# Hooks of the large products moved one product earlier inside a block

## The chip, the cores and the metric

The kernel runs on one core of a Trainium2 chip. The metric is device time in microseconds (us) of one execution; the number that counts is the median of several runs. "Fast" here means fewer microseconds, nothing else. Differences are told against the kernel before the change.

## The reference

The program is one inference step of a two-layer backbone with width 2048. It treats 128 context tokens and 128 latent tokens together, so nearly every matrix product has 256 token columns. Cut to what matters here, a layer is:

```python
mod = silu(cond) @ w_ada[l] + b_ada[l]           # shift, scale, gate, twice
h = rmsnorm(x, g_norm_mix[l]) * (1 + sc1) + sh1
m = mixer_ab(h, ...) if l % 2 == 0 else mixer_c(h, ...)   # attention, in and out products
x = x + gt1 * m
h = rmsnorm(x, g_norm_ffn[l]) * (1 + sc2) + sh2
x = x + gt2 * conv_ffn(h, ...)                   # w_up 2048 x 11264, w_down 5632 x 2048
```

Layer 0 has the mixer of two head groups, layer 1 the differential attention (`mixer_c`). All weights are float32 and are read once from device memory.

## The kernel before, in words

Tokens lie in the columns and features in the partitions. A large product is made block column by block column: 128 output features at a time, over `KD = 16` blocks `k` of 128 input features, all added up in one PSUM tile `acc`. For precision every operand is split into a high and a low part in the type fp32r. The weights come by DMA as `raw` tiles of 1 MB; ScalarE writes the high part `wh` (L237) and VectorE the low part `wl` (L238). The inputs `hx`, `hxc` or `u` hold their high part `xh(k)` and low part `xl(k)` side by side. One block `k` is thus three matmuls: `wh.xh`, `wh.xl` and `wl.xh`. In the profile's rows the first two read the tile `wh` and the third reads `wl`; all of TensorE's matmuls bear the line L104 of a helper, its transposes L107, so they are told apart by tile names.

`gemm` writes these 48 matmuls of one output block. It takes an argument `between`: a function, called at block 8 of 16, or a table from block number to function. What such a hook issues stands in the middle of a block's three matmuls. Where `between` is given, all the matmuls of the product are kept in the order in which they are written (`keep_order`); hooks issue their own TensorE instructions into the same order. There are three users:

- `modulated`, called three times, makes the first three block columns of the next large product out of inputs that are not normalised yet (`u`, 258 columns wide: the two extra ones carry the shift). Its hooks are the sums of the norm (`stats`, at block 6 of the first product: four matmuls into an `att` tile), the spreading of the resulting factor over all partitions (`factor`, block 13 of the first), and the two halves of one unit of the `w_ada` product (`sums(0)` at block 6 of the second product, `sums(2)` at block 13 of the third: 8 matmuls each out of two `araw` tiles).
- `ffn` passes a table for its first products; one of them holds a hook with the four transposes that end such a unit (`misc<-am`).
- `mixer_c` passes `middle` with each of its projections. It pumps one step of whatever is due: the scores of a head (`att<-dk,dq`), transposes, the products with the values (`att<-dv,pT`), rows of `w_ada` (`ada<-araw`), and side sums on VectorE (`aacc<-block`, L481) whose 256 KB tiles `block` come over the same DMA queue (SP, L497) as the weights (SP, L284).

Instructions of the other engines are placed by a scheduler that works through a simulated timeline, under the same chain of kept orders where `keep_order` pins them. Buffers come from rotating pools: three `raw` tiles of 16 blocks, four `wh` and four `wl` halves of 8 blocks, three `acc`, three `att`, three `block`.

Of the kernel before, what the change touches and what calls it, by code (L numbers as in the profile page):

```python
# [88 lines left out]
def step_kernel(ctx: ExitStack, tc: tile.TileContext, A: dict):  # L89
# [4 lines left out]
    def keep_order(i):  # L94
        if not any(i is j for j in kept):
            kept[:] = [i]
            tc.keep_in_program_order(i)
# [16 lines left out]
    pe = TensorE()  # L114
# [20 lines left out]
    def T_(pl, shape, tag, dt=F32, bufs=None):  # L135
        kw = {} if bufs is None else {"bufs": bufs}
        return pl.tile(shape, dt, tag=tag, name=nm(tag), **kw)
# [185 lines left out]
    def gemm(blocks, xh, xl, n=NT, first=0, between=None):  # L323

        fixed = lambda i: keep_order(i) if between is not None else i
        ps = T_(pacc, [P, 512], "acc")
        last = len(blocks) - 1
        for i in range(last + 1):  # L330
            k = (i + first) % (last + 1)
            wh, wl = blocks[k]
            fixed(pe.matmul(ps[:, :n], wh, xh(k), start=(i == 0), stop=False))
            fixed(pe.matmul(ps[:, :n], wh, xl(k), start=False, stop=False))
            if callable(between):
                if i == (last + 1) // 2:
                    between()
            elif between and i in between:
                between[i]()
            fixed(pe.matmul(ps[:, :n], wl, xh(k), start=False, stop=(i == last)))  # L340
        return ps[:, :n]

# [323 lines left out]
    def modulated(st, l, which, W, u, to, rp):  # L666
# [39 lines left out]
        hooks[2][13] = lambda: sums(2)  # L706
        uh, ul = (lambda k: u[:, k, :UW]), (lambda k: u[:, k, UW:])
        ps = [gemm(W.chunk(), uh, ul, UW, between=hooks[c]) for c in range(2)]
        last = W.chunk()
        rb = got["rb"]  # L710
# [4 lines left out]
        for c in range(KD):  # L715
# [3 lines left out]
            if c in (5, 10):  # L719
                W.ahead(lambda i: i)  # L720
        ready.append(scaled(gemm(last, uh, ul, UW, between=hooks[2]), rbs))
        if which == 0:
            later.extend(steps)
# [119 lines left out]
    def mixer_ab(hx, rb0, beside):  # L843
        l = 0
        with tc.tile_pool(name="ab", bufs=1) as ab:
            with tc.tile_pool(name="abp", bufs=1) as pj:
# [105 lines left out]
                def part(W, k0, n, first, rate, between=None, then=None, **kw):  # L952

                    for c in range(23):
                        ps = gemm(W.chunk(), lambda k: hx[:, k0 + k, :NT], lambda k: hx[:, k0 + k, NT:2 * NT])
                        to = pr[:, c] if c < 11 else kvb[:, c - 11] if c < 15 else qb[:, c - 15]
                        if first:
                            act.copy(to, ps)
                        else:
                            dve.tensor_tensor(out=to, in0=to, in1=ps, op=ALU.add)  # L960
                        if between:
                            between(c)
                        pump(rate, **kw)
                        if c == 18 and then:
                            then()
# [542 lines left out]
```

## Time and profile before

| | |
|---|---|
| runs | 2368.92 us median of 3 (2361.41, 2368.92, 2373.19) |
| the profiled execution | 2368.09 us, of it 2366.2 us span from first to last instruction |
| TensorE matmul busy | 2324.9 us (98% of the span), 19666 matmuls |
| VectorE, ScalarE, GpSimd busy | 1852.1, 1191.0, 177.8 us |
| mean granted TensorE clock | 0.995 |
| DMA | 612.97 MB, mean 259 GB/s |

The stages in the profile's time, us from the start of the span: input products, heads and output product of layer 0 up to 455; first `modulated` about 455 to 492; feed-forward of layer 0 to 1180; second `modulated` to 1210; `mixer_c` to about 1500, its output product to 1604; third `modulated` to 1638; feed-forward of layer 1 to the end. A row of the timeline gives start, duration, engine, line, operation, tiles and count; "PE" is a matmul, "PEld" the load of its stationary operand.

### The profile page before, as it was taken

The page shows a single profiled execution, that of the slowest core. Times are in us where ns is not written, and L with a number is a line of the kernel's source. Part 1 is how long each engine was busy: PE and PEld are TensorE (multiplying, and loading weights), DVE is VectorE, ACT ScalarE, POOL GpSimd, SP SyncE. Part 2 cuts the span into 40 slices and gives each one's busy share as a digit, 9 for nine tenths or more (in the row PEclk, how much of TensorE's full clock was granted, in tenths as well). Part 3 has the DMA queues.
Part 4 walks back from the last instruction along what each step waited for, and adds up shares of the span by engine and source line. Part 5 has one row for each costly group of instructions (what it writes and reads, how often), then busy time and mean ns, then how long its engine had stood idle before and what let it go on. Part 6 is the DMA issues. An engine that isn't in the chain of part 4 may idle for free.

```text
span 2366.2 us, 47897 instructions
## 1 busy us (share of the span) xinstructions
PE 2324.9 (98%) x19666; PEld 2214.9 (94%) x19666; DVE 1852.1 (78%) x2864; ACT 1191.0 (50%) x1980; POOL 177.8 (8%) x242
## 2 busy tenths in 40 slices
PE   6999999999999999999999999999999999999998
PEld 4788778999999999999999999999999999999998
DVE  3569768889999999999988888787998655666644
ACT  4246455665553355554564544557555434555443
POOL 0002111210000000001130000123000000000011
PEclk9999999999999999999999999999999999999999
DMA  9988888677777777677778888667666555555553
GB/s 362 354 320 302 300 301 333 233 281 267 266 256 291 288 280 260 251 264 276 281 277 305 291 292 313 246 250 267 250 250 246 181 191 183 188 187 186 189 183 121
DMA packets 106812, 612.97 MB, mean 259 GB/s; under 512 B 11553, under 2 KB 19553, under 8 KB 38881
## 3 DMA queue, kind: packets, MB, share of 16 engines
q1 hardware_dynamic: 106592, 609.92, 70.8%
q8 instruction: 154, 2.52, 0.4%
q14 instruction: 66, 0.53, 0.1%
HBM read 605.12 MB, written 4.75 MB: 258 GB/s over the span
## 4 chain that ended last, share of the span: by engine, by line
PE 95%; DVE 2%; DMA 2%; ACT 1%; issue 0%; POOL 0%; DVEq 0%; ACTq 0%
PE acc L104 87%; PE ada L104 4%; PE att L104 2%; DMA araw<-w_ada 1%; PE att L107 1%; DVE wl L238 1%; PE misc L104 0%; PE ada L107 0%; DMA raw<-w_in_ab 0%; DVE sqacc L200 0%; DVE x L1370 0%; DMA cst<-cst 0%; ACT wh L237 0%; DVE aacc L481 0%; DMA block<-w_ada 0%
## 5 line engine op out<-in xcount | busy, mean ns | idle before, releaser
L104 PE MATMUL acc<-hx,wh 128*128 128x256 f32 (+1 forms) x7296 | 1278.8, 280 | 6.6 <-ACT hx L614 4.3
L237 ACT CAST wh<-raw 128x1024 fp32r<-128x1024 f32 (+2 forms) x824 | 793.5, 974 | 956.8 <-PE acc L104 758.5
L238 DVE TENSOR_TENSOR wl<-raw,wh 128x1024 fp32r<-128x1024 f32 (+2 forms) x824 | 920.8, 1132 | 312.3 <-ACT wh L237 309.6
L104 PEld LDWEIGHTS acc<-hx,wh 128*128 128x128 f32 x7296 | 1109.1, 188 | 37.3 <-issue 17.1
L104 PE MATMUL acc<-hx,wl 128*128 128x256 f32 (+1 forms) x3648 | 1017.2, 279 | 4.7 <-DVE wl L238 4.7
L104 PEld LDWEIGHTS acc<-hx,wl 128*128 128x128 f32 x3648 | 692.4, 190 | 7.7 <-DVE wl L238 5.9
L104 PE MATMUL acc<-g,wh 128*128 128x256 f32 x2816 | 488.2, 278 | 0.0
L104 PEld LDWEIGHTS acc<-g,wh 128*128 128x128 f32 x2816 | 426.9, 188 | 0.0
L104 PE MATMUL acc<-g,wl 128*128 128x256 f32 x1408 | 391.7, 279 | 0.0
L452 DVE CUSTOM_DVE_ANT_0 junk<-araw,condb 128x2048 f32<-128x2048 f32 x120 | 275.8, 2298 | 0.0
L104 PE MATMUL acc<-hxc,wh 128*128 128x256 f32 (+1 forms) x1536 | 267.8, 278 | 0.2 <-DVE hxc L741 0.2
L104 PEld LDWEIGHTS acc<-g,wl 128*128 128x128 f32 x1408 | 267.2, 190 | 0.0
L104 PEld LDWEIGHTS acc<-hxc,wh 128*128 128x128 f32 x1536 | 233.3, 188 | 0.7 <-DVE hxc L741 0.4
L104 PE MATMUL acc<-hxc,wl 128*128 128x256 f32 (+1 forms) x768 | 218.2, 284 | 0.0
L200 POOL TENSOR_TENSOR sqacc<-sqacc,sq 128x256 f32<-128x256 f32 x62 | 70.8, 1143 | 1539.9 <-ACT sq L196 1533.4
L481 DVE SCALAR_TENSOR_TENSOR aacc<-block,condw,aacc 128x512 f32<-128x512 f32 x240 | 172.0, 753 | 11.1 <-DMA block<-w_ada 10.9
L104 PEld LDWEIGHTS acc<-hxc,wl 128*128 128x128 f32 x768 | 144.7, 188 | 8.7 <-issue 5.4
L104 PE MATMUL ada<-araw,condw 128*32 128x512 f32 (+1 forms) x736 | 92.6, 598 | 15.9 <-ACT sq L196 12.7
L1262 ACT ACTIVATE cv<-acc,convw 128x256 f32<-128x256 f32 x170 | 95.0, 559 | 0.0
L773 DVE SCALAR_TENSOR_TENSOR x<-acc,mod,x 128x128 f32<-128x128 f32 x190 | 57.4, 343 | 39.8 <-PE acc L104 39.7
L1268 DVE SCALAR_TENSOR_TENSOR cv<-acc,convw,cv 128x254 f32<-128x254 f32 x170 | 81.3, 478 | 3.3
L1265 DVE SCALAR_TENSOR_TENSOR cv<-acc,convw,cv 128x254 f32<-128x254 f32 x170 | 80.6, 474 | 0.0
(229 smaller groups left out, 1400.8 us busy)
## 6 DMA issues: line engine op xcount, KB each, us to landing
raw<-w_up SPq DMA_DIRECT2D x176, 1024.0 KB, 4.8
araw<-w_ada SPq DMA_DIRECT2D x146, 1024.0 KB, 6.1
raw<-w_down SPq DMA_DIRECT2D x88, 1024.0 KB, 4.8
raw<-w_in_c SPq DMA_DIRECT2D x48, 1024.0 KB, 6.9
block<-w_ada SPq DMA_DIRECT2D x128, 256.0 KB, 5.7
raw<-w_in_ab SPq DMA_DIRECT2D x19, 1024.0 KB, 7.4
raw<-w_out_ab SPq DMA_DIRECT2D x16, 1024.0 KB, 7.1
raw<-w_out_c SPq DMA_DIRECT2D x16, 1024.0 KB, 5.4
```

The lines of the kernel that those rows point to most:

```text
L104: return self.placed(nc.tensor.matmul(*a, **kw))
L107: return self.placed(nc.tensor.transpose(*a, **kw))
L200: eng.tensor_tensor(out=st["acc"], in0=st["acc"], in1=sq, op=ALU.add)
L237: pin(act.copy(out_hi, src))
L238: pin(dve.tensor_tensor(out=out_lo, in0=src, in1=out_hi.bitcast(F32), op=ALU.subtract))
L452: keep_order(dve.tensor_tensor_reduce(out=T_(feat["pool"], [P, D], "junk"), in1=feat["row"][:, c], in0=feat["raw"].rearrange("p g n -> p ( ...
L481: i = dve.scalar_tensor_tensor(out=acc[c], in0=block, scalar=condw[:, k, c:c + 1], in1=acc[c], op0=ALU.mult, op1=ALU.add)
L773: dve.scalar_tensor_tensor(out=x[:, c, s], in0=ps[:, s], scalar=mod[:, l, 3 * which + 2, c, g:g + 1], in1=x[:, c, s], op0=ALU.mult, op1=AL ...
L1262: pin(act.activation(y, ps, AF.Identity, scale=cw[:, 1, m:m + 1], bias=cw[:, 3, m:m + 1]))
L1265: pin(dve.scalar_tensor_tensor(out=y3[:, :, 1:], in0=p3[:, :, :T - 1], scalar=cw[:, 0, m:m + 1], in1=y3[:, :, 1:], op0=ALU.mult, op1=ALU.add))
L1268: pin(dve.scalar_tensor_tensor(out=y3[:, :, :T - 1], in0=p3[:, :, 1:], scalar=cw[:, 2, m:m + 1], in1=y3[:, :, :T - 1], op0=ALU.mult, op1=A ...
```

## The change

In `gemm` the second matmul of a block, `wh.xl`, moves from ahead of the hook to behind it. A hook so stands behind the first matmul of the block instead of behind the second. Products without a hook, and blocks without one, are written as before.

```diff
             fixed(pe.matmul(ps[:, :n], wh, xh(k), start=(i == 0), stop=False))
-            fixed(pe.matmul(ps[:, :n], wh, xl(k), start=False, stop=False))
             if callable(between):
                 if i == (last + 1) // 2:
                     between()
             elif between and i in between:
                 between[i]()
+            fixed(pe.matmul(ps[:, :n], wh, xl(k), start=False, stop=False))
             fixed(pe.matmul(ps[:, :n], wl, xh(k), start=False, stop=(i == last)))
```

In the built program 48 matmuls change their place on TensorE: 34 in `mixer_c`, 12 in the three calls of `modulated`, 2 in the two feed-forward stages. On TensorE nothing else moves. The scheduler also sets 19 instructions of VectorE, 11 of ScalarE, 3 of GpSimd and 7 transfers of SP elsewhere in their queues, all of them between the second `modulated` and the start of the output product of `mixer_c`. No instruction but a few bare semaphore events is added or dropped, and all buffers keep their addresses. Here is TensorE in `mixer_c`, at the hook that issues the scores of the first head (`hxc` are the inputs, `dk` and `dq` the head's keys and queries). Before:

```order
L104 MATMUL acc_14819<-hxc_14493,wl_14812 128x256
L104 MATMUL acc_14819<-hxc_14493,wh_14815 128x256 x2
L104 MATMUL att_14848<-dk_14674,dq_14673 128x128
L104 MATMUL att_14848<-dk_14674,dq_14673 128x256
L104 MATMUL att_14858<-dk_14674,dq_14673 128x128
L104 MATMUL att_14858<-dk_14674,dq_14673 128x256
L104 MATMUL acc_14819<-hxc_14493,wl_14816 128x256
```

And after, at the same place:

```order
L104 MATMUL acc_14819<-hxc_14493,wl_14812 128x256
L104 MATMUL acc_14819<-hxc_14493,wh_14815 128x256
L104 MATMUL att_14847<-dk_14674,dq_14673 128x128
L104 MATMUL att_14847<-dk_14674,dq_14673 128x256
L104 MATMUL att_14857<-dk_14674,dq_14673 128x128
L104 MATMUL att_14857<-dk_14674,dq_14673 128x256
L104 MATMUL acc_14819<-hxc_14493,wh_14815 128x256
L104 MATMUL acc_14819<-hxc_14493,wl_14816 128x256
```

The second matmul with `wh` went from ahead of the four score matmuls to behind them; the one with `wl` stays behind them in both.

On SP's queue the order of weights (`raw`) and side blocks (`block`) changes in a few places. This is the first, at the start of `mixer_c`, before:

```order
L497 DMA block_14951<-w_ada 128x512
L497 DMA block_15025<-w_ada 128x512
L284 DMA raw_14988<-w_in_c 128x2048
L497 DMA block_15029<-w_ada 128x512
L1149 DMA o_diff_k<-dk_14674 128x2x128
```

And after:

```order
L497 DMA block_14950<-w_ada 128x512
L497 DMA block_15024<-w_ada 128x512
L497 DMA block_15028<-w_ada 128x512
L284 DMA raw_14988<-w_in_c 128x2048
L1149 DMA o_diff_k<-dk_14674 128x2x128
```

One weight tile went behind a side block. A second such pair stands further on in `mixer_c`; in four more places an output transfer (`o_diff_k`) goes behind a side block.

## The prediction

> **What bounds the kernel now.** I read the page first, then the busy time by stretches for the places where the change moves something, then the waits and the timeline there. The page says that TensorE is the bound nearly everywhere: it is busy for 98% of the span, and the chain that ended last runs through it for 95%.
>
> ```profile
> PE 2324.9 (98%) x19666; PEld 2214.9 (94%) x19666; DVE 1852.1 (78%) x2864; ACT 1191.0 (50%) x1980; POOL 177.8 (8%) x242
> PE 95%; DVE 2%; DMA 2%; ACT 1%; issue 0%; POOL 0%; DVEq 0%; ACTq 0%
> ```
>
> An average says little about the places that are touched. The next rows are the stretches that hold all 48 moved matmuls: the first `modulated` and the first feed-forward products behind it (450 to 510), the second `modulated` (1183 to 1210), `mixer_c` (1210 to 1500), the third `modulated` and what follows (1604 to 1660). The columns are the length, busy time and instructions of each engine, the granted clock, the DMA engines' busy share and GB/s.
>
> ```profile
> 450.00:492.00 42.00, 42.00 (x361) 38.85 (x359) 34.88 (x73) 33.08 (x75) 18.60 (x26) 1.00 0.74 282
> 492.00:510.00 18.00, 18.00 (x161) 18.00 (x160) 12.79 (x21) 13.37 (x16) 0.00 (x0) 1.00 0.62 221
> 1183.00:1210.00 27.00, 26.17 (x218) 22.51 (x217) 23.25 (x46) 20.53 (x52) 18.99 (x25) 1.00 0.82 303
> 1210.00:1500.00 290.00, 290.00 (x2457) 272.93 (x2456) 244.78 (x397) 145.18 (x287) 15.10 (x28) 1.00 0.84 294
> 1604.00:1638.00 34.00, 34.00 (x291) 30.85 (x290) 28.43 (x58) 27.79 (x62) 17.69 (x25) 1.00 0.81 319
> 1638.00:1660.00 22.00, 22.00 (x189) 22.00 (x188) 16.23 (x23) 14.86 (x18) 0.00 (x0) 1.00 0.63 225
> ```
>
> TensorE is busy without a break in all of them but one, and at the full clock (1.00). In `mixer_c` that is 290.00 of 290.00 us. Only the second `modulated` has idle time, 27.00 - 26.17 = 0.83 us, and TensorE's waits of that stretch name it: a transfer of `araw` and a row of `hxc`. The columns are total, times, longest.
>
> ```profile
> PE ada L104 <- DMA araw<-w_ada: 0.6, 1, 0.6
> PE acc L104 <- DVE hxc L741: 0.2, 1, 0.2
> ```
>
> A busy engine can still hide a slow start inside modelled ends, so I looked at one hook itself, the scores of the first head, in the timeline.
>
> ```profile
> 1218.15 0.39 PE L104 MATMUL acc<-hxc,wh 128*128 128x256 f32 x2
> 1218.26 1.18 PEld L104 LDWEIGHTS att<-dk,dq 128*128 128x128 f32 x8
> 1218.38 1.47 PE L104 MATMUL att<-dk,dq 128*128 128x128 f32 x8
> 1219.47 0.19 PEld L104 LDWEIGHTS acc<-hxc,wl 128*128 128x128 f32 x1
> 1219.50 0.47 PE L104 MATMUL acc<-hxc,wl 128*128 128x256 f32 x1
> 1219.80 0.40 PE L104 MATMUL acc<-hxc,wh 128*128 128x256 f32 x2
> ...
> 1387.59 10.90 PE acc L104 x96
> ```
>
> The last row, from the chain of waits, gives the pace of the large products: 10.90 / 96 = 0.1135 us from one start to the next. The two matmuls with `wh` begin at 1218.15 and about 1218.26, the small ones at 1218.38, that is one product time behind the second. So the hook joins the stream on the beat. On the other side the small ones' last load is over when `wl` is loaded at 1219.47, and the stream goes on. The hook costs its own work and no gap that an order could save.
>
> **The change, part by part.** The profiled execution took 2368.09 us, 0.83 us below the median of the three runs (2368.92); I add up changes against the former and give the result against the latter.
>
> *The moved matmul.* Each of the 48 hooks starts one large product earlier, 0.1135 us, and the product that stood ahead of it runs behind it. The work is the same. If what the hook reads is ready, TensorE ends the block at the same moment: 48 x 0 = 0. If it isn't, the hook waits up to 0.1135 us more than now, and the product that used to cover this comes later: at most 48 x 0.1135 = 5.4 us. On the other side there is nothing to win but the idle time that the stretches show: at most 0.83 us. I take 0, since the stretch that holds 34 of the 48 hooks shows no wait whatever before them (290.00 of 290.00), so that readiness leads by an amount that one product will not use up. What follows from a hook also comes 0.1135 us earlier for ScalarE and VectorE; they are not the bound, so this is worth 0 too.
>
> At `sums(2)` of the second `modulated`, where TensorE waits 0.6 us for `araw`, the two ends of the chain move together: the transfer is issued when `sums(0)` has freed the buffers, which comes 0.1135 us earlier, and it is asked for 0.1135 us earlier. The wait stays as it is.
>
> *The stationary operand.* The two products with `wh` no longer stand next to each other at a hook. If the hardware kept `wh` loaded between them, the change would add 48 loads. Here are the matmuls of `mixer_c` with `wh` and their loads.
>
> ```profile
> L104 PE MATMUL acc<-hxc,wh 128*128 128x256 f32 (+1 forms) x1536 | 267.8, 278 | 0.2 <-DVE hxc L741 0.2
> L104 PEld LDWEIGHTS acc<-hxc,wh 128*128 128x128 f32 x1536 | 233.3, 188 | 0.7 <-DVE hxc L741 0.4
> ```
>
> There are 1536 loads for 1536 matmuls: both products of a block load `wh` already, side by side or not. So no load is added, and 0 is taken. If 48 loads of 188 ns were added and nothing covered them, that would be 48 x 0.188 = 9.0 us. The Trainium skill, "TensorE: Matmul & The Clock Gate", under "Step-by-step: what each phase is for", says that the separate load lets one load the weights once and multiply with them repeatedly, which speaks against parting two products of the same weights. By that page's figure for a load (columns / 1.2 GHz, here about 107 ns) an estimate of the loss would be 48 x 0.107 = 5.1 us. By that rule the change costs; the trace does not agree that this program uses it, with its 1536 loads for 1536 matmuls.
>
> *ScalarE, VectorE and GpSimd.* Their reordered rows lie mostly where `hxc` is made, in the second `modulated`. There `hxc` is late by 0.2 us at one place; the last row of it on VectorE and a typical row of ScalarE in its chain are these.
>
> ```profile
> 1208.83 0.41 DVE L741 TENSOR_TENSOR hxc<-block,hxc 128x256 fp32r<-128x256 f32 x1
> 1200.71 0.49 ACT L735 ACTIVATE block<-block,mod,scl 128x128 f32<-128x128 f32 x1
> ```
>
> VectorE's row moves ahead of a `wl` cast that stood before it, which favours it; up to three of ScalarE's rows go ahead of a cast of `hxc` and could delay it by 3 x 0.49 = 1.5 us. I take 0, between a gain of 0.2 and a loss of 1.5, as the wait is nearest to the 0.2 us that the row shows.
>
> *SP's queue.* Two weight tiles and four outputs go behind a side block. The side block waits for its buffer, so that what is behind it is issued later. These are SP's longest kinds of wait in `mixer_c`, then how long a weight tile takes to land, then how ScalarE waits with the weights' cast.
>
> ```profile
> SPq L497 <- DVE aacc L481: 79.0, 51, 4.7
> SPq L284 <- DVE wl L238: 61.1, 33, 5.5
> raw<-w_in_c SPq DMA_DIRECT2D x40, 1024.0 KB, 7.0
> ACT wh L237 <- PE acc L104: 113.9, 75, 3.9
> ```
>
> The worst wait of a side block is 4.7 us, the mean 79.0 / 51 = 1.5 us. For the weights it matters only if it is longer than their lead. A product uses one tile in 48 x 0.1135 = 5.45 us, and three tiles rotate, so that a buffer comes round again after 3 x 5.45 = 16.3 us; less 7.0 us for the landing and some 5.45 us in which its two halves are cast, 3.9 us of lead are left at the DMA, and the cast halves give more: ScalarE waits 75 times for TensorE to release one, 1.5 us on average, before it may cast the next. A mean wait of 1.5 us is covered twice. I take 0; without any cover the two weight tiles would cost 2 x 4.7 = 9.4 us. The outputs feed nobody in this stretch until their buffers are needed again.
>
> The sum is 0, between -0.8 - 0.2 = -1.0 us and 5.4 + 1.5 = 6.9 us where the two costs with the least cover in the trace add up. Against the median that is 2368.9 us.
>
> **The rivals.**
>
> *No cover for the hooks* (slower, inside 0.5%). Each hook waits out what it gained: 2368.9 + 5.4 = 2374.3 us; with the load of 188 ns exposed instead, 2377.9 us. Against it speak 290.00 us busy of 290.00 us and the equal counts of loads and matmuls. For it: the releases of `att` scores by ScalarE are inferred, not shown. Chance 0.14.
>
> *The weights lose their lead in `mixer_c`* (slower). The six places where a transfer goes behind a side block each hold SP for the longest wait seen there, 4.7 us, and the loss does not come back because the DMA engines are busy for 0.84 of that stretch: 6 x 4.7 = 28.2 us, 2397.1 us; half of it gives 2383.0 us. It decides from where a wait exceeds the 3.9 us of lead and what the cast halves add. Two of the six places carry weights, and at the first of them the side block followed the weight tile by only about a microsecond. Chance 0.10.
>
> *The stream gets looser* (faster). The earlier results of the hooks let VectorE, 84% busy in `mixer_c`, end its work sooner. But TensorE has only 0.83 us to give there: 2368.1 us. What would show as more than 0.5% faster is not this mechanism but something that the profile of before does not hold. Chance 0.08, half of it beyond 0.5%.
>
> **How the numbers follow.** A difference of 0.5%, 11.8 us, is about what a measurement of this kernel can tell from no change: the three runs before span 2373.19 - 2361.41 = 11.78 us. The forecast, no change, has 0.68, the rivals 0.14, 0.10 and 0.08. The forecast leaves 0.03 to each side beyond 0.5% by the scatter of runs alone. Faster: 0.03 + 0.04 = 0.07. Slower: 0.03 + 0.09 of the second rival + 0.02 of the first = 0.14. The rest, 0.79, is within 0.5%. The range reaches from the lowest run less the largest gain, 2361.4 - 1.0 = 2360.4, to the highest run with the hooks' waits, 2373.2 + 5.4 = 2378.6: 2360 to 2379 us. It holds the forecast and the first rival, and leaves out most of the second.
>
> **What would show it.** In the profile after, the stretch 1210 to 1500 should again have TensorE busy for its whole length, the matmuls and loads of `hxc` with `wh` should again be 1536 each at the same means, and 0.1135 us should stay the pace. TensorE's waits in the second `modulated` should stay below 2 us. Wrong would be: waits of `att` or `ada` matmuls for ScalarE in `mixer_c` (first rival); waits of ScalarE's weight casts for `raw<-w_in_c`, and of TensorE for `wh` or `wl` (second); or a changed clock or pace in stages whose order did not change.

## The result and the profile after

The changed kernel takes 2364.91 us, the median of 12 runs (2361.15 to 2369.59). The kernel before, with 12 runs in all by now, takes 2364.95 us (2361.41 to 2373.19). The ratio is 0.9999 with a 95% interval of 0.9987 to 1.001: no difference that can be measured.

The profiled execution took 2362.23 us (span 2360.4), 5.9 us less than that of before. The chain of waits shows that most of this is not the change. Its two longest rows are the feed-forward stages; the columns are start, duration, engine and tile, line, count. Before:

```profile
492.70 690.34 PE acc L104 x6090
1638.61 714.93 PE acc L104 x6070
```

After:

```profile
488.02 690.34 PE acc L104 x6090
1632.56 715.04 PE acc L104 x6071
```

The first feed-forward takes 690.34 us in both, to a hundredth of a microsecond. But it starts 4.68 us earlier after the change. Of that, 4.52 us are there at the row of the chain that starts at 422.04 us before and at 417.52 us after, ahead of the first stage that the change touches. The stages up to there scatter by that much from one execution to the next: in the profiles of all the runs below, the first feed-forward starts between 485.84 and 496.44 us, and both ends of that range come from kernels with the changed hooks. The second starts 6.05 us earlier, so 1.4 us were won between the two.

Two of the stretches that the prediction showed, at the same times in the profile after:

```profile
1183.00:1210.00 27.00, 27.00 (x231) 23.85 (x230) 25.42 (x49) 22.51 (x56) 18.80 (x24) 1.00 0.81 306
1210.00:1500.00 290.00, 290.00 (x2454) 272.85 (x2453) 244.85 (x399) 145.09 (x292) 14.08 (x30) 1.00 0.83 290
```

`mixer_c` again keeps TensorE busy for its whole length. The stretch at the second `modulated` now has no idle time either; the 0.6 and 0.2 us of waits of the first profile before are gone in this one. The groups of `hxc` with `wh` on the page after:

```profile
L104 PE MATMUL acc<-hxc,wh 128*128 128x256 f32 (+1 forms) x1536 | 276.6, 281 | 0.0
L104 PEld LDWEIGHTS acc<-hxc,wh 128*128 128x128 f32 x1536 | 235.9, 188 | 8.7 <-issue 8.4
```

The counts are equal as before, and so is the mean of a load. The mean of the matmuls is 281 ns instead of 278, where the prediction had expected the same. The products with `wl` go the other way, from 284 to 278 ns: the profile records the product right behind a hook as a long one (0.47 us in the prediction's timeline), and that is now one with `wh`. The two 690 and 715 us rows hold one more thing, which the prediction had passed over in the profile of before and which the experiments brought up: 690.34 / 6090 = 113.4 ns for a product in the first feed-forward, but 714.93 / 6070 = 117.8 ns in the second, for the same matmuls on a TensorE that is busy 100% in both.

### The profile page after: what moved, and what is told of

Same layout as the page of the kernel before. It is cut to its first block, busy times and chain, and to the rows that moved or that the text cites. A ratio compares the mean times of both kernels' runs of the same rounds, so it can differ in the third digit from the quotient of the medians.

```text
span 2360.4 us, 47894 instructions
## 1 busy us (share of the span) xinstructions
PE 2323.6 (98%) x19666; PEld 2214.8 (94%) x19666; DVE 1850.4 (78%) x2864; ACT 1191.4 (50%) x1980; POOL 176.7 (7%) x242
## 4 chain that ended last, share of the span: by engine, by line
PE 96%; DVE 2%; DMA 1%; ACT 1%; issue 0%; SPq 0%; POOL 0%; DVEq 0%; ACTq 0%
PE acc L104 88%; PE ada L104 4%; PE att L104 2%; PE att L107 1%; PE misc L104 1%; DVE wl L238 1%; DMA araw<-w_ada 0%; PE ada L107 0%; ACT wh L237 0%; DMA raw<-w_in_ab 0%; DVE x L1370 0%; DVE aacc L481 0%; DVE nt L604 0%; DMA block<-w_ada 0%; DVE proj L960 0%
## 5 line engine op out<-in xcount | busy, mean ns | idle before, releaser
L104 PE MATMUL acc<-hxc,wh 128*128 128x256 f32 (+1 forms) x1536 | 276.6, 281 | 0.0
```

Of the source, the lines that this page charges most:

```text
L104: return self.placed(nc.tensor.matmul(*a, **kw))
```

## The experiments

**Both kernels once more.** No edit.

> The kernel before, unchanged, for a second profile. Theory (the change is worth nothing but at most the idle time of the second modulated): all stages from the first modulated on take the same time as in its first profile to within 0.2 us, except the second modulated, where TensorE's waits may be anything from 0 to 1.5 us because they hang on when a transfer of araw lands. The difference of several us between two executions lies in the first 300 us. Rival (the change removes the waits of the second modulated): TensorE waits there again for araw and for hxc, 0.8 us together, as in the first profile.

> The changed kernel, unchanged, for a second profile. Theory: mixer_c (1210 to 1500 in the profile before) has TensorE busy throughout; the second modulated shows 0 to 1.5 us of waits, not necessarily the 0 of the first profile. Rival (the change removes these waits): 0 again, and about 1.3 us less from the feed-forward of layer 0 to the end than in both profiles of the kernel before.

The totals were 2370.45 us (before) and 2362.63 us (after). The rows of the chain of waits, before again, then after again:

```profile
494.91 690.34 PE acc L104 x6090
1640.97 714.93 PE acc L104 x6070
```

```profile
486.73 690.34 PE acc L104 x6090
1632.96 715.04 PE acc L104 x6071
```

From one feed-forward's start to the other's it is 1146.06 us here and 1145.91 in the first profile before, against 1146.23 here and 1144.54 after. So the 1.4 us of the first profile after did not come back. TensorE's waits at the second `modulated` are part of this: before again (first fence) has both waits, after again (second) has that for `araw` but not that for `hxc`.

```profile
PE ada L104 <- DMA araw<-w_ada: 0.6, 1, 0.6
PE acc L104 <- DVE hxc L741: 0.2, 1, 0.2
```

```profile
PE ada L104 <- DMA araw<-w_ada: 0.7, 1, 0.7
```

The 0.2 us for `hxc` are missing in both profiles after and there in both before, as the reordered row of VectorE would have it; the 0.6 us for `araw` hang on the transfer and come and go. The waits are not the whole of it. From the first profile after to the second, the time between the two feed-forwards grew by 1.69 us: 0.87 us up to the end of the stretch with the wait for `araw`, then 0.52 us because the 129 products behind it take 15.41 us instead of 14.89, 0.68 us because 159 products of `mixer_c`'s output product take 18.99 us instead of 18.31, less twice 0.2 us in stretches of 48 products. The program is the same, and all its instructions stand in the same order in both traces. So the pace of a stretch can differ from one execution to the next, which the theory's 0.2 us for a stage did not allow for. On the totals the theory holds, with a gain of 0.2 us at `hxc` that no timing can see.

**The two products of `wh` never side by side.** In all blocks of `gemm`, against the kernel before:

```diff
-            fixed(pe.matmul(ps[:, :n], wh, xl(k), start=False, stop=False))
+            fixed(pe.matmul(ps[:, :n], wl, xh(k), start=False, stop=False))
             ...
-            fixed(pe.matmul(ps[:, :n], wl, xh(k), start=False, stop=(i == last)))
+            fixed(pe.matmul(ps[:, :n], wh, xl(k), start=False, stop=(i == last)))
```

> The kernel before with the second and third matmul of every block of gemm exchanged: wh.xh, wl.xh, hook, wh.xl. Two products with the same wh never stand next to each other, some 6000 times instead of 48. Theory (every matmul has a load of its own, hidden behind the matmul before it): 0.1135 us a product as before, total within 0.5% of the kernel before, a few us at most for wl being needed one product earlier. Rival (wh stays loaded between neighbours, or its second load is cheaper): at 0.107 to 0.188 us for each of about 6000 pairs, 640 to 1130 us slower.

It took 2343.9 us: not 640 to 1130 us slower, but 21 us faster. The rows of the chain of waits:

```profile
495.77 690.36 PE acc L104 x6090
1640.91 687.98 PE acc L104 x6070
```

The first feed-forward parts some 2000 pairs and costs 690.36 us instead of 690.34. That settles the question of the load: neighbours with the same weights share nothing here. The rule of the Trainium skill that the prediction weighed ("TensorE: Matmul & The Clock Gate", "Step-by-step: what each phase is for": load once, multiply repeatedly) is not what this stream of load and matmul pairs does, and the run shows it 2000 times over. But the second feed-forward fell from 714.93 to 687.98 us, 113.3 ns a product, which nobody had expected.

**The hooks one product later.** Against the kernel before:

```diff
             fixed(pe.matmul(ps[:, :n], wh, xl(k), start=False, stop=False))
-            if callable(between):
-            ...
             fixed(pe.matmul(ps[:, :n], wl, xh(k), start=False, stop=(i == last)))
+            if callable(between):
+            ...
```

> The hook one product later than in the kernel before, behind the third matmul of its block: the opposite direction of the change. Theory: TensorE is busy throughout mixer_c, total within 0.5% of before, stages after the first 450 us the same to about 1.5 us. Rival (the place of the hook inside a block matters): the opposite sign of whatever the change did, by about as much, a few us.

It took 2334.43 us, over 1% below any run of the kernel before; both the theory and its rival were wrong on the total. Up to the third `modulated` all stages were as expected. The gain lies in one row:

```profile
1631.94 687.85 PE acc L104 x6069
```

That is 27 us less than 714.93 us, again at 113.3 ns a product. Over several executions:

> All hooks behind the third matmul, again, now timed against the kernel before in five rounds, since the first look gave 2334.4 us. Theory A (TensorE's large products run at one of two paces, 113.3 or 117.8 ns a product; which one is set anew behind every group of small matmuls and then holds; the feed-forward of layer 1 runs at 117.8 in the kernels before and after and at 113.3 here, some 6070 x 4.5 ns = 27 us): ratio 0.987 with an interval of less than 0.3%. Rival (the first look was a lucky execution): 0.998 to 1.002.

Median 2336.49 us against 2364.11 us, ratio 0.9878 (0.9858 to 0.9898). It is no lucky execution.

**How much cover the hooks have.** Two runs with the hooks of the changed kernel that are passed as functions, which are all of `mixer_c`'s (and the feed-forward's), at an earlier block:

```diff
-                if i == (last + 1) // 2:
+                if i == 4:        # and 0 in the second run
```

> The changed kernel, with mixer_c's hook at block 4 instead of 8: 12 products or 1.36 us earlier, twelve times the step of the change. Theory (what the hooks read is ready by more than that): mixer_c has TensorE busy throughout, total within 0.5%. Rival (readiness leads by little): waits of TensorE for ScalarE or VectorE at the att or misc matmuls, up to 34 x 1.36 = 46 us.

> The changed kernel, with mixer_c's hook at block 0: 24 products or 2.72 us earlier than the change has it, right behind the first matmul of a product. Now the transposes of a head's values read what ScalarE copies out of the product that has just ended (0.36 us and its queue). Theory: this takes the cover away: TensorE waits 0.5 to 1.5 us once a head for dev, 4 to 12 us over mixer_c, and the other hooks still wait for nothing. Rival (the cover is larger still): no wait, mixer_c unchanged. Other rival (all hooks have little cover): up to 34 x 2.72 = 92 us.

They took 2371.28 and 2373.82 us; the kernel before took 2368.41 us beside them. TensorE's waits in `mixer_c`, hook at block 4, then at block 0:

```profile
PE att L107 <- ACT dev L1155: 0.7, 1, 0.7
PE att L104 <- DVE dk L791: 0.4, 1, 0.4
```

```profile
PE att L107 <- ACT dev L1155: 6.7, 7, 1.0
PE att L104 <- DVE dk L791: 0.4, 1, 0.4
```

Twelve products earlier than in the changed kernel cost 1.1 us in two waits, not quite the nothing that was expected; 24 products earlier cost 7.1 us, one wait of about 1 us for each of seven heads, inside the 4 to 12 us expected and for the reason named: the transposes wait for ScalarE's copy of the product that has just ended. So the step of the change, one product, lies far inside the cover.

**How much lead the weights have.** Fewer buffers for the side blocks of `mixer_c` and for the pairs of rows in `modulated` of layer 1, in the changed kernel, so that SP stands longer at a side block:

```diff
-        block = T_(side["pool"], [P, 512], "block", bufs=3)
+        block = T_(side["pool"], [P, 512], "block", bufs=2 if side["apart"] else 3)   # and 1
...
-                pair = T_(rp, [P, 512], "block", bufs=3)
+                pair = T_(rp, [P, 512], "block", bufs=2 if l else 3)   # and 1
```

> The changed kernel with two buffers instead of three for the side blocks of mixer_c (and for the pairs of rows in the two modulated calls of layer 1), so that SP waits longer at a side block and holds the weights behind it. Theory (the weights' lead covers a wait of up to about 4 us): TensorE still busy throughout mixer_c or nearly, under 5 us lost. Rival (the lead is nearly used up): ScalarE's weight casts wait for raw, TensorE idle, 10 to 30 us slower.

> As the run with two buffers for the side blocks, with one: each side block is asked for only when the one before has been used, some 5.3 us landing and 1.4 us on VectorE, for about 80 blocks in 290 us. Theory: SP in its order now holds the weights by more than their lead; ScalarE waits for raw, TensorE for wh, 80 x 6.7 = 540 us for the side blocks instead of 290, so up to 250 us slower, all of it in mixer_c and its output product. Rival (a side block held on SP doesn't reach the products at all): no change in mixer_c.

With two buffers it took 2385.3 us, 17 us above the kernel before beside it. From one feed-forward's start to the other's it is 1159.14 us, against 1144.54 to 1146.23 us in the four profiles above, so 13 to 15 us of this are the edit's. With one buffer it took 2473.88 us, 105 us above, and 1253.08 us between the two starts. The size of the first is that of its rival, but the way is mostly another. In `mixer_c`, ScalarE's casts of the weights waited for TensorE and not for `raw` in both runs. TensorE's longest wait in `mixer_c`, two buffers, then one:

```profile
PE att L104 <- DVE dk L791: 3.9, 3, 2.4
```

```profile
PE misc L104 <- DVE aacc L481: 46.8, 3, 27.1
```

What a late side block holds up there is VectorE's sum `aacc`: between 1210 and 1500 us it waits 30.6 us for `block` with two buffers and 69.6 us with one, against 9.4 us in the kernel before. Behind that stands whatever follows in VectorE's queue (`dk`) or in TensorE's own order (`misc<-aacc`). The weights kept their lead in the projections of `mixer_c`, but not behind them: for the first tiles of its output product, ScalarE's casts waited up to 5.0 and 4.6 us for `raw<-w_out_c`, against 0 and 2.0 us in the two profiles of the kernel before. With two buffers, the 7.00 us landing of such a tile lies in the chain that ended last. So the prediction's slow rival had the wrong victim in `mixer_c`, and the right one just behind it.

TensorE's waits from the second `modulated` to the second feed-forward add up to 9.2 us with two buffers and to 85.8 us with one, less than what was lost. The granted clock was lower too: 0.99 and 0.90 in 1210 to 1500, against 1.00 before and after. How much of the rest that explains was not separated.

**Which hook sets the pace.** Two parts of the 27 us version, each on top of the changed kernel, with a helper `hook(i)` that holds the old branch. The test tells the users apart because `modulated` passes its hooks in tables, while `mixer_c` and `ffn` pass theirs as functions (the tables of `ffn`, other than the text ahead says, hold no hook):

```diff
+        late = callable(between) and not pe.in_turn         # e10: the feed-forward's hooks
+        late = bool(between) and not callable(between)      # e11: modulated's hooks
...
             fixed(pe.matmul(ps[:, :n], wh, xh(k), start=(i == 0), stop=False))
+            if not late:
+                hook(i)
             fixed(pe.matmul(ps[:, :n], wh, xl(k), start=False, stop=False))
             fixed(pe.matmul(ps[:, :n], wl, xh(k), start=False, stop=(i == last)))
+            if late:
+                hook(i)
```

> The changed kernel, with only the hooks of the two feed-forward stages (four transposes each) behind the third matmul of their block, all others behind the first. Theory B (the place of the last hook inside its block sets the pace of the whole feed-forward of layer 1): it runs at 113.3 ns a product there, 27 us faster than the changed kernel. Rival C (what counts is the pace that the stream has when it comes to the hook, set by the hooks ahead of it in modulated): still 117.8 ns, no change.

> The changed kernel, with only modulated's twelve hooks behind the third matmul, those of the feed-forward stages and of mixer_c behind the first. Rival C: the stream comes to the hook of the feed-forward of layer 1 at 117.8 ns and leaves it at 113.3, 27 us faster than the changed kernel. Theory B: 117.8 ns behind the hook as in the changed kernel, no change.

The feed-forward's hooks alone: 2363.91 us, ratio 0.9991 (0.9977 to 1.0004), no change. `modulated`'s hooks alone: 2336.89 us, ratio 0.9881 (0.9857 to 0.9904), all of the gain. The second feed-forward, first run, then second:

```profile
1634.46 714.81 PE acc L104 x6069
```

```profile
1632.23 688.09 PE acc L104 x6071
```

Theory B falls, rival C stands. The last run narrows it to one hook:

```diff
+        if isinstance(between, dict) and list(between) == [13]:
+            lasts[0] += 1
+            late = lasts[0] == 3
+        else:
+            late = False
```

> The changed kernel with one hook of the 48 behind the third matmul of its block: the last hook of the third modulated (the second half of a w_ada unit, block 13 of the third product). Theory C1 (the hook that comes last ahead of the feed-forward's hook decides the pace at which the stream comes to it): 117.8 ns a product between the two hooks, 113.3 behind the second, the feed-forward of layer 1 27 us faster, ratio to the kernel before 0.988. Rival C2 (the earlier hooks of modulated are needed for it): 113.3 ns between the hooks and 117.8 behind, ratio 0.999 to 1.001.

Median 2336.0 us against 2365.97 us, ratio 0.9882 (0.986 to 0.9904). One hook of 48, placed two products later than in the changed kernel, is worth 29 to 30 us in the medians (against 2364.91 and 2365.97 us), and 27 us in the row of the second feed-forward (688.09 against 715.04 us). In the two traces nothing else differs: every engine has its instructions in the same order, but for these two products on TensorE and their loads. Here are 12 us ahead of the feed-forward's hook and 12 us behind it, in the kernel before, the changed kernel and this one; the number in the first brackets counts the matmuls that run in the window, with those that only reach into it.

```profile
1625.00:1637.00 12.00, 12.00 (x109) 12.00 (x108) 10.99 (x19) 11.21 (x19) 1.43 (x2) 1.00 0.99 403
1640.00:1652.00 12.00, 12.00 (x105) 12.00 (x104) 7.72 (x13) 9.09 (x11) 0.00 (x0) 1.00 0.62 217
```

```profile
1619.00:1631.00 12.00, 12.00 (x108) 12.00 (x107) 10.99 (x19) 11.22 (x19) 1.45 (x2) 1.00 0.98 392
1634.00:1646.00 12.00, 12.00 (x104) 12.00 (x104) 7.74 (x14) 9.04 (x11) 0.00 (x0) 1.00 0.66 223
```

```profile
1618.00:1630.00 12.00, 12.00 (x105) 12.00 (x104) 11.02 (x20) 10.89 (x17) 0.33 (x1) 1.00 1.00 414
1633.00:1645.00 12.00, 12.00 (x109) 12.00 (x108) 7.23 (x10) 8.96 (x10) 0.00 (x0) 1.00 0.62 230
```

Before and after, the stream comes to the four transposes at the fast pace (108 or 109 matmuls in 12 us) and leaves them at the slow one (104 or 105). With the hook ahead of it moved, it comes slow and leaves fast. The busy time is 12.00 of 12.00 us and the clock 1.00 in all six. And then it stays so to the end of that stage, in which no small matmul follows but at its end:

```profile
1630.95 688.09 PE acc L104 x6071
```

This is the version that beats both kernels; it and the ones with 12 and 48 moved hooks lie within 1 us of each other, so the single hook accounts for the whole gain.

## Why the prediction was right

**The moved matmul at 0: right.** `mixer_c` is 290.00 of 290.00 us busy again, and with the hook at block 4 all but two hooks find their operands ready twelve products earlier.

**The stationary operand at 0: right**, shown with every pair of `gemm` parted.

**The reordered rows of VectorE and ScalarE at 0, between a gain of 0.2 and a loss of 1.5 us: right**, with the gain of 0.2 us in both profiles after. The low end of the prediction's sum counts these 0.2 us twice, since the 0.83 us of idle time already hold them. The wait for `araw` staying as it is: right in one profile after, gone in the other, so it belongs to the scatter.

**SP's queue at 0: right.** In the profile after, no cast of ScalarE in `mixer_c` waits for `raw`. The rival was priced on the weights' lead, and in `mixer_c` the weights kept it even with one buffer; what suffers there from a late side block are VectorE's sums. The weights came late only at the output product behind `mixer_c`, and most with fewer buffers.

**The forecast of no change: right, but in part by luck.** Two steps of the prediction failed without harm. It took one pace, 0.1135 us, for all large products, from a row of `mixer_c`. Another row of the same chain, also in `mixer_c`, has 117.8 ns for the same 96 products:

```profile
1226.38 11.31 PE acc L104 x96
```

The second feed-forward runs at 117.8 ns too, as its row of 714.93 us for 6070 products says to whoever divides it. The very hook that the prediction looked at, and behind which it saw no gap, turns the fast pace into the slow one: the 48 products behind it take 5.65 us in the chain, 117.7 ns each. And it said that there is nothing to win but the 0.83 us of idle time in the touched stretches. A TensorE that is busy without a break can still go 4% slower, and the order decides: moved one product the other way, the same hooks win 28 us. The rival that was given 0.08, a faster stream by something the profile does not hold, was the one nearest to a real effect; it needs another place of one hook.

The prediction did not argue that every long stage would keep its pace, and no row of the profile before shows that it would, so that part was luck. The profiles show only that it came so: in `mixer_c` both paces come up many times, with changes at hooks, and from 1226 us of the profile before up to the output product the stretches of 48 and 96 products repeat one by one, to 0.01 us, in all four profiles of the two kernels.

## What to carry to other kernels

Divide time by instructions for each long stretch of a stream, and compare stretches that do the same work: busy shares of 100% hid 27 us here, and two rows of the chain of waits showed them. A move of small instructions inside a stream that never waits is worth what the waits of that place are worth, unless it changes the rhythm that the stream falls into behind them; here only trying found it, at one hook in front of a long stage. Execution times that differ by several microseconds are best compared stage by stage, since here everything behind the first 300 us repeats to less than 2 us of some 2060 within each kernel's two profiles.

## What the runs showed of the hardware

Pairs of a 128x128 weight load and a 256-column fp32r matmul run back to back at one of two paces, 113.3 or 117.8 ns a pair. Both have the same clock: the granted clock is 1.00 in all six windows around the feed-forward's hook. The Trainium skill, "TensorE: Matmul & The Clock Gate", "What's actually happening", knows a half and a full rate of the gated clock; the trace agrees that neither stretch was gated, so this is something else. In one stage a pace holds over 6000 pairs and 690 us, through other engines' work and transfers. Most changes of pace in the profiles stand behind a group of small matmuls. A wait can do it too: in both profiles of the kernel before, the stream comes to TensorE's 0.2 us wait for `hxc` at the fast pace, but the same 79 products behind it take 9.24 us in the first and 9.57 us in the second.

In the second feed-forward the pace repeats: the two profiles of the kernel before, the two of the changed kernel and the two with all hooks later each show the same one there (714.93 twice, 715.04 twice, 687.85 and 687.86 us). It is not fixed by the program everywhere: the 129 products at the end of the second `modulated` took 14.89 us in one profile of the changed kernel and 15.41 us in the other, behind a wait for `araw` that only the second had.

There is not one rule for a group either. In the kernel before, the four transposes ahead of the second feed-forward turn fast into slow (129 products in 14.89 us ahead of them, 6070 in 714.93 us behind). Ahead of the first they leave the fast stream fast (129 in 14.88 us, then 6090 in 690.34 us). What in TensorE keeps the pace, and what in a group decides it, stays open. The runs show which hook sets it, not how.
